# A two-layer hybrid transformer trunk on one core: Strassen's form for the first MLP product of layer 0

## The chip, the core and the metric

The kernel runs on 1 core of one Trainium2 chip. The metric is the device time of one execution in microseconds (us); of several runs the median is taken. Engines: PE is TensorE (matmuls; PEld its weight loads), DVE is VectorE, ACT is ScalarE, POOL is GpSimd, SP is SyncE, which here issues nearly all DMAs. SBUF is the on-chip memory that all engines read, PSUM the memory that matmuls write.

## What is computed

Two layers of a trunk of width 1024 over 512 noised (latent) tokens and 256 context tokens. Cut to what matters here:

```python
for l in range(2):
    m_lat, m_ctx = silu(c) @ w_mod[l] + b_mod[l], silu(c_ctx) @ w_mod[l] + b_mod[l]   # 6 x 1024 each
    h = modulate(rmsnorm(x), sh1, sc1)            # latent and context each with their own
    x = x + ga1 * (concat(attention(h), gated_mlp(h)) @ w_out[l])
    h = modulate(rmsnorm(x), sh2, sc2)
    x = x + ga2 * (square(relu(h @ w_ff1[l])) @ w_ff2[l])     # 1024 -> 4096 -> 1024
return x_lat                                       # in layer 1 only the latent part goes on after attention
```

The change concerns the last line of layer 0, over all 768 tokens: `h @ w_ff1` is called the first product, the one with `w_ff2` the second.

## The kernel before

All activations lie feature-major: 8 tiles of 128 features x 768 tokens. Matmuls are 128x128 weights by up to 512 tokens in fp32r. For precision each operand is split into a rounded part hi (a cast on ACT, L207) and the rest lo (a subtraction on DVE, L208), and each product takes three matmuls: hi·hi, hi·lo, lo·hi. A token run of 768 is done in two halves of 384, so that an output tile of the first product (8 feature blocks, 3 matmuls, 2 halves) takes 48 matmuls of 128x384.

**Weights.** Blocks of 128x1024 come in a fixed order (`block_order`): a DMA on SP's queue into one of two raw buffers, a split into a ring of 4 hi and 4 lo slots (`pump`, `split`). `take` hands a block to its user, `release` frees it, and later `settle` pumps the next.

**Layer 0's MLP.** The 32 hidden tiles are made in 8 chunks of 4 and live in eight units of SBUF, B0 to B6 and C0. `ff1` (L986) makes one tile: 48 matmuls into a PSUM tile pa, then `relu2`: Relu on ACT (L954), Square on ACT (L959) to hi, a square (L960) and a subtraction (L961) on DVE to lo. The second product of a chunk (`proj4`, L786) takes the four hidden tiles, makes 8 output tiles m0 to m7 (24 matmuls each, in turn in pa, or in pb and pt), and each is added to the residual X with the modulation's gate on DVE (`gate`, L784: 384 columns of the first half, then 128 and 256 of the second). The tiles of chunk c+1 are made around the second product of chunk c: one ahead of it, three behind. So each chunk has 384 matmuls, 192 for either product.

**Beside it.** `mod_wide` (L347) computes layer 1's modulation, without PE: 128x512 blocks of w_mod come by DMA, ACT multiplies by the condition (L365, L368), POOL adds (L369); DVE transposes and sums (L380, L381). The MLP calls `more()` to emit a piece of it at a time. `consts(1)` (L550) loads layer 1's small constants and builds its rotary tables (L563, L564); it is called after `ff1_first`, the first chunk of layer 0.

**Order.** In chunks 0 to 6 the instructions of DVE and ACT keep the order in which the program is written (`manual_schedule`, "DA"); a scheduler orders those of PE, POOL and SP, and in chunk 7 all of them. An instruction waits for its inputs on its own engine's queue, and all behind it wait with it. The program's waits on PSUM go by whole tiles.

## Time and profile before

| | |
|---|---|
| median of 3 runs | 1532.02 us (1531.33 to 1533.99) |
| span of the profiled execution | 1530.9 us |
| the stretch of layer 0's MLP taken for the stage | 433 to 911 us |
| instructions | 22786 |

The page gives, for the slowest (here the only) core, each engine's busy time, the chain of work that ended last, and groups of instructions by source line, engine, operation and tile names (`out<-in`). Matmuls are pipelined, so that the row of one shows more (0.33 us) than the distance to the next. Waits are put down to what came last before the waiting instruction began.

### The profile page before, as it was taken

To read this page: it belongs to the slowest core of one execution; us is meant where nothing else is said; L and a number is where in the kernel's file an instruction comes from. 1 tells how busy PE (TensorE), PEld (TensorE's weight loads), DVE (VectorE), ACT (ScalarE), POOL (GpSimd) and SP (SyncE) were. 2 spreads that over 40 slices of the span, in tenths; PEclk is the share of its full clock that TensorE was granted. 3 is DMA by queue.
4 is the path that set the end of the run, shared out by engine and by line. 5 is a ranking of instruction groups with operands and counts; after the bars stand their busy time and mean duration, and the time that the engine had idled before them with its cause. 6 is when DMAs were issued, how large, how long until landed. Compare 5 with 4: busy or idle time off the path is not lost.

```text
span 1530.9 us, 22786 instructions
## 1 busy us (share of the span) xinstructions
PE 1484.1 (97%) x8804; PEld 1321.5 (86%) x8804; DVE 957.4 (63%) x1874; ACT 682.6 (45%) x1142; POOL 402.0 (26%) x362
## 2 busy tenths in 40 slices
PE   6999899999999999999999999998999999999998
PEld 2899686779899999999999998996889888888887
DVE  5868966776855555555555547988796644444443
ACT  3542355564545453545444424535784433322221
POOL 0112320023244545545454603035213000000000
PEclk9999999999999999999999999999999999999999
DMA  9221324321134333333333321221101333332332
GB/s 359 67 74 48 119 91 152 110 83 56 62 108 122 113 123 126 111 118 106 124 109 124 98 68 56 86 80 44 41 1 56 97 96 97 98 97 97 96 98 79
DMA packets 49948, 148.83 MB, mean 97 GB/s; under 512 B 5424, under 2 KB 6832, under 8 KB 49840
## 3 DMA queue, kind: packets, MB, share of 16 engines
q1 hardware_dynamic: 49264, 146.46, 29.9%
q8 instruction: 69, 1.13, 0.3%
q10 hardware_dynamic: 576, 0.92, 0.2%
q14 instruction: 39, 0.32, 0.1%
HBM read 145.26 MB, written 2.10 MB: 96 GB/s over the span
## 4 chain that ended last, share of the span: by engine, by line
PE 82%; DVE 12%; DMA 2%; ACT 2%; issue 1%; POOL 0%; SPq 0%; ACTq 0%; POOLq 0%; DVEq 0%
PE pa L203 51%; PE pb L203 21%; PE pt L844 3%; PE pt L203 3%; PE pb L326 2%; DVE lo L208 1%; DMA X<-in_xT 1%; DMA C<-in_w_mod 1%; DVE X L784 1%; DMA A<-in_w_mod 1%; DVE m L277 1%; PE pt L626 1%; DVE B L961 1%; ACT hi L207 1%; PE pb L865 0%
## 5 line engine op out<-in xcount | busy, mean ns | idle before, releaser
L203 PE MATMUL pa<-A,hi 128*128 128x384 f32 (+2 forms) x1696 | 449.2, 347 | 1.7 <-ACT w L954 0.6
L207 ACT CAST hi<-raw 128x1024 fp32r<-128x1024 f32 x171 | 179.5, 1050 | 409.9 <-PE pa L203 326.3
L208 DVE TENSOR_TENSOR lo<-raw,hi 128x1024 fp32r<-128x1024 f32 x155 | 202.7, 1308 | 215.8 <-ACT hi L207 212.4
L203 PEld LDWEIGHTS pa<-A,hi 128*128 128x128 f32 x1696 | 304.7, 188 | 25.9 <-ACT w L954 1.8
L369 POOL TENSOR_TENSOR C<-C,s 128x512 f32<-128x512 f32 x168 | 240.5, 1463 | 245.0 <-ACT s L368 244.8
L203 PE MATMUL pa<-A,lo 128*128 128x384 f32 (+2 forms) x848 | 293.4, 347 | 1.1 <-DVE lo L208 1.1
L203 PE MATMUL pa<-B,hi 128*128 128x384 f32 (+1 forms) x900 | 246.4, 356 | 4.4 <-DVE X L784 4.4
L203 PEld LDWEIGHTS pa<-B,hi 128*128 128x128 f32 x900 | 162.9, 188 | 21.5 <-DVE X L784 9.2
L784 DVE SCALAR_TENSOR_TENSOR X<-pa,modT,X 128x384 f32<-128x384 f32 (+1 forms) x168 | 88.0, 547 | 143.0 <-PE pa L203 143.0
L203 PEld LDWEIGHTS pa<-A,lo 128*128 128x128 f32 x848 | 159.3, 188 | 12.0 <-DVE lo L208 1.3
L203 PE MATMUL pa<-B,lo 128*128 128x384 f32 (+1 forms) x450 | 158.1, 353 | 0.0
L203 PE MATMUL pb<-B,hi 128*128 128x256 f32 (+2 forms) x600 | 152.3, 340 | 0.4 <-DVE X L784 0.4
L368 ACT ACTIVATE s<-k,silu 128x512 f32<-128x512 f32 x168 | 114.3, 716 | 49.4 <-DMA k<-in_w_mod 27.3
L203 PE MATMUL pb<-hi,A 128*128 128x256 f32 x672 | 126.1, 285 | 0.0
L784 DVE SCALAR_TENSOR_TENSOR X<-pb,modT,X 128x512 f32<-128x512 f32 (+3 forms) x116 | 69.1, 602 | 75.8 <-PE pb L203 75.3
L203 PEld LDWEIGHTS pb<-B,hi 128*128 128x128 f32 x600 | 104.0, 189 | 11.6 <-DVE X L784 1.0
L203 PEld LDWEIGHTS pb<-hi,A 128*128 128x128 f32 x672 | 106.1, 191 | 0.2 <-issue 0.2
L203 PE MATMUL pb<-B,lo 128*128 128x256 f32 (+2 forms) x300 | 101.5, 338 | 0.0
L203 PE MATMUL pb<-lo,A 128*128 128x256 f32 x336 | 95.3, 284 | 0.0
L203 PEld LDWEIGHTS pa<-B,lo 128*128 128x128 f32 x450 | 84.4, 188 | 5.8
L847 DVE TENSOR_TENSOR A<-pt,A 128x384 fp32r<-128x384 f32 (+1 forms) x144 | 73.6, 535 | 16.4 <-ACT A L846 14.4
L846 ACT CAST A<-pt 128x384 fp32r<-128x384 f32 (+1 forms) x144 | 64.6, 469 | 43.3 <-PE pt L844 39.5
(169 smaller groups left out, 2300.3 us busy)
## 6 DMA issues: line engine op xcount, KB each, us to landing
raw<-in_w_ff SPq DMA_DIRECT2D x128, 512.0 KB, 3.5
k<-in_w_mod SPq DMA_DIRECT2D x96, 256.0 KB, 3.0
hi<-in_w_mod SPq DMA_DIRECT2D x32, 512.0 KB, 3.6
raw<-in_w_tok SPq DMA_DIRECT2D x19, 512.0 KB, 3.5
raw<-in_w_out SPq DMA_DIRECT2D x16, 512.0 KB, 3.5
A<-in_w_mod SPq DMA_DIRECT2D x8, 512.0 KB, 9.9
raw<-in_w_u SPq DMA_DIRECT2D x8, 512.0 KB, 3.5
B<-in_w_mod SPq DMA_DIRECT2D x6, 512.0 KB, 10.2
```

The source lines that it names most:

```text
L203: pe.matmul(out, a, b, start=start, stop=stop)
L207: act.copy(hi, src)
L208: (eng or vec).tensor_tensor(out=lo, in0=src, in1=hi.bitcast(F32), op=ALU.subtract)
L277: vec.tensor_scalar(yi, v.bitcast(I32), -0.5, 1595932665.0, op0=ALU.mult, op1=ALU.add)
L326: pe.matmul(ps[q:q + 32, :], S32[:, k, :], w[:, k2 * 512:(k2 + 1) * 512], start=k < ns, stop=k >= KT - ns)
L368: act.activation(p, w, AF.Copy, scale=s)
L369: pool_e.tensor_tensor(out=a, in0=a, in1=p, op=ALU.add)
L626: pe.transpose(p[:, o:o + 128], stk[:, t, hh, c0:c0 + 128].bitcast(F32), ident)
L784: vec.scalar_tensor_tensor(out=xs, in0=src[:, s - off:e - off], scalar=modT[l][:, i * 8 + m, cond:cond + 1], in1=xs, op0=ALU.mult, op1=ALU ...
L844: pe.transpose(tp_[:, (kt - k0) * 128:(kt - k0) * 128 + 128], p[:, kt * 128:kt * 128 + 128], ident)
L846: act.copy(pth[:, k0:k0 + step, d], src)
L847: vec.tensor_tensor(out=ptl[:, k0:k0 + step, d], in0=src, in1=pth[:, k0:k0 + step, d].bitcast(F32), op=ALU.subtract)
```

## The change

In layer 0, chunks 1 to 7, the first product is made in pairs of hidden tiles (p, p + 16) by Strassen's scheme in Winograd's form: the two tiles' weights are split into 2 x 2 blocks of 4 x 128 rows (A11, A12 of tile p, A21, A22 of tile p + 16), the tokens into two halves of 384 and the features into two halves of four blocks (B11 to B22). Instead of 8 block products, 7 are taken (12 matmuls of 128x384 each), of sums of blocks. Chunk 0 is made as before, from tiles 0, 16, 1, 17, and w_ff2's rows are re-ordered on the host to match.

- `factor` makes the weight factors one ring slot at a time: al (the raw A11, A12), be (S2 and S1), ga (what has become of A11 and A12), q (a half slot of its own). POOL computes them in place by four additions of 128x512 (L288 to L291) on the raw buffer and on a second buffer in unit B6 or C0. 3.5 blocks are split for each pair instead of 2.
- `factors` makes the token sums, once, issued under chunk 0's second product: 8 additions of 128x768 on POOL (hi + lo, L1085), 16 differences on DVE (L1096), 16 hi on ACT, 8 lo on DVE and 8 on POOL (L1098). They are kept in units B0 to B5 and in the token half of the first four h tiles that they replace.
- `ff1_pair` (L1120) takes the 7 products in PSUM halves A and C (one pa tile), B (pb) and E (pt), and combines them on ACT and DVE. Its products in order: A1 (al), C1 (be), A2 (al), B1 (be), E (q), B2 (ga), C2 (ga). `c1_` and `c5` are copies of A1 and C1 out of PSUM.
- Hidden tiles now lie in four units, H0 to H3, which at other times hold other data (layer 1's constants in H2 and H3), so both pairs of a chunk are made ahead of its second product, and none runs a chunk ahead. `proj4` with `early` does the first half of the contraction for m0 to m2 first.
- `consts(1)` is called at the end of chunk 7.
- `mod_wide` leaves out the context condition for the column blocks j from 4 on, which layer 1 doesn't use: 112 additions on POOL instead of 168. Its last step is put off by 6000 ns of the emission clock, and `more()` is called at other places (none in chunk 0's second product).

In the whole program there are 168 matmuls of 128x384 fewer (2976, then 2808), 122 more tensor_tensor and 42 more scalar_tensor_tensor on DVE, 86 more casts and 92 fewer activations on ACT, 30 more tensor_tensor on POOL, and as many DMAs (335).

```diff
+        if l == 0:
+            o += [("ff1", l, m) for m in (0, 16, 1, 17)]
+            for ch in range(8):
+                if ch:
+                    a, b = 2 * ch, 2 * ch + 1
+                    o += [("al", l, a), ("be", l, a), ("al", l, b), ("ga", l, a), ("be", l, b), ("ga", l, b)]
+                o += [("ff2", l, ch, nb) for nb in range(4)]
+            continue
...
+    def factor(key):
+        kind, l, p = key
+        hi, lo = slot()
+        if kind == "al":
+            ra = ring.tile([128, 1024], F32, tag="raw", name=nm("raw"), bufs=2)
+            nc.sync.dma_start(ra, w_ff1[l, p])
+            rb = unit(("B6", "C0")[p % 2], [128, 1536], F32)
+            nc.sync.dma_start(rb[:, 512:1536], w_ff1[l, p + 16])
+            raws[p] = ra, rb
+            split(hi, lo, ra)
+            a11, a12, s2, a21, a22 = ra[:, 0:512], ra[:, 512:1024], rb[:, 0:512], rb[:, 512:1024], rb[:, 1024:1536]
+            tt = pool_e.tensor_tensor
+            tt(out=a11, in0=a11, in1=a21, op=ALU.subtract)
+            tt(out=a21, in0=a21, in1=a22, op=ALU.add)
+            tt(out=s2, in0=a22, in1=a11, op=ALU.subtract)
+            tt(out=a12, in0=a12, in1=s2, op=ALU.subtract)
+        elif kind == "be":
+            split(hi, lo, raws[p][1][:, 0:1024])
+        else:
+            ra, rb = raws.pop(p)
+            split(hi, lo, ra)
+            qh, ql = (ring.tile([128, 512], F32R, tag=t, name=nm(t), bufs=1) for t in ("qh", "ql"))
+            split(qh, ql, rb[:, 1024:1536])
+            ready.append((("q", l, p), qh, ql))
+        ready.append((key, hi, lo))
...
+            conds = range(2 if j < 4 else 1)
...
+                    if early and pi == 0 and m < 3:
+                        if m == 0:
+                            wbs.update((i, take(*keys, i)) for i in range(2))
+                            ew = [w4(wbs[i // 2], i, R) for i in range(3)]
+                            if len(parts) > 1:
+                                ed = [pa(), None, pa()]
+                                ed = [[p[:, 0:512], p[:, 512:1024]] if p is not None else [pb(), pt()] for p in ed]
+                            else:
+                                p = pa()
+                                ed = [[p[:, 0:512]], [p[:, 512:1024]], [pb()]]
+                            for i in range(3):
+                                for q, (off, n) in enumerate(parts):
+                                    fm_mms(ed[i][q][:, 0:n], ew[i], off, n, 0, 2)
+                                fl.tick()
+                        for q, (off, n) in enumerate(parts):
+                            fm_mms(ed[m][q][:, 0:n], ew[m], off, n, 2, 4)
+                            gate(i_, m, off, n, ed[m][q])
+                            if post:
+                                post(m, off)
+                            if pi == len(passes) - 1 and q == len(parts) - 1 and m % 2:
+                                release()
+                            yield
+                        continue
...
+        strassen = l == 0
+        hn = TQ // 2
+        def hidden(m):
+            H[m] = unit(f"H{(m % 2) + m // 16 * 2}" if strassen else hslots[m % 8], [128, 2, T])
...
+        def factors():
+            ux = [unit(f"B{i}", [128, 2, 2, 384]) for i in range(6)]
+            def tokens(k):
+                hv = []
+                for kk in (k, k + 4):
+                    v = tw([128, TQ])
+                    pool_e.tensor_tensor(out=v, in0=h2[kk][:, 0, 0:TQ].bitcast(F32), in1=h2[kk][:, 1, 0:TQ].bitcast(F32), op=ALU.add)
+                    hv.append(v)
+                return hv
+            for k in range(4):
+                hv = tokens(k)
+                b11, b12, b21, b22 = hv[0][:, 0:hn], hv[0][:, hn:TQ], hv[1][:, 0:hn], hv[1][:, hn:TQ]
+                dst = [h2[k][:, :, hn:TQ]] + [ux[(k * 3 + i) // 2][:, (k * 3 + i) % 2] for i in range(3)]
+                TT.append(dst)
+                t = [None] * 4
+                for i, (x, y) in ((0, (b12, b11)), (1, (b22, 0)), (3, (b21, 1)), (2, (b22, b12))):
+                    t[i] = tsm([128, hn])
+                    vec.tensor_tensor(out=t[i], in0=x, in1=t[y] if isinstance(y, int) else y, op=ALU.subtract)
+                    act.copy(dst[i][:, 0], t[i])
+                    (pool_e if i > 1 else vec).tensor_tensor(out=dst[i][:, 1], in0=t[i], in1=dst[i][:, 0].bitcast(F32), op=ALU.subtract)
+                    yield
...
+        def put(m, j, sq):
+            hi, lo = (H[m][:, a, j * hn:(j + 1) * hn] for a in range(2))
+            act.copy(hi, sq)
+            vec.tensor_tensor(out=lo, in0=sq, in1=hi.bitcast(F32), op=ALU.subtract)
+        def sqrelu(t):
+            vec.scalar_tensor_tensor(out=t, in0=t, scalar=0.0, in1=t, op0=ALU.max, op1=ALU.mult)
+            return t
...
+        def ff1_pair(p):
+            hidden(p)
+            hidden(p + 16)
+            quad = lambda j, n: lambda k: tuple(h2[j * 4 + k][:, a, n * hn:(n + 1) * hn] for a in range(2))
+            tsum = lambda i: lambda k: tuple(TT[k][i][:, a, 0:hn] for a in range(2))
+            ps = pa()
+            A, C = ps[:, 0:hn], ps[:, 512:512 + hn]
+            B, E = pb()[:, 0:hn], pt()[:, 0:hn]
+            cc = tw([128, 2, hn])
+            uu = tw([128, 2, hn])
+            c1_, c5 = cc[:, 0], cc[:, 1]
+            U2, U3 = uu[:, 0], uu[:, 1]
+            tt = vec.tensor_tensor
+            al = take("al", l, p)
+            product(A, al, 0, quad(0, 0), True, True)
+            act.copy(c1_, A)
+            be = take("be", l, p)
+            product(C, be, 512, tsum(0), True, True)
+            act.copy(c5, C)
+            more()
+            product(A, al, 512, quad(1, 0), False, True)
+            release()
+            r = tsm([128, hn])
+            act.activation(r, A, AF.Relu)
+            hd = H[p]
+            act.activation(hd[:, 0, 0:hn], r, AF.Square)
+            tt(out=r, in0=r, in1=r, op=ALU.mult)
+            tt(out=hd[:, 1, 0:hn], in0=r, in1=hd[:, 0, 0:hn].bitcast(F32), op=ALU.subtract)
+            more()
+            product(B, be, 0, tsum(1), True, True)
+            release()
+            tt(out=U2, in0=B, in1=c1_, op=ALU.add)
+            more()
+            product(E, take("q", l, p), 0, tsum(3), True, True)
+            ga = take("ga", l, p)
+            product(B, ga, 0, tsum(2), False, True)
+            tt(out=U3, in0=B, in1=c1_, op=ALU.add)
+            pool_e.tensor_tensor(out=c5, in0=c5, in1=U3, op=ALU.add)
+            t21 = tsm([128, hn])
+            tt(out=t21, in0=E, in1=U3, op=ALU.add)
+            put(p + 16, 0, sqrelu(t21))
+            more()
+            product(C, ga, 512, quad(1, 1), False, True)
+            release()
+            tt(out=U2, in0=C, in1=U2, op=ALU.add)
+            put(p, 1, sqrelu(U2))
+            put(p + 16, 1, sqrelu(c5))
+            more()
...
-        if not last:
-            K1.append(consts(l + 1))
...
-                    ff1(ch * 4 + 4)
-                    more()
-                R = [H.pop(ch * 4 + kk) for kk in range(4)]
+                if strassen:
+                    if ch:
+                        ff1_pair(2 * ch)
+                        ff1_pair(2 * ch + 1)
+                    R = [H.pop(m) for m in (2 * ch, 2 * ch + 16, 2 * ch + 1, 2 * ch + 17)]
+                    sums = factors() if ch == 0 else iter(())
+                else:
+                    if ch < 7:
+                        ff1(ch * 4 + 4)
+                    R = [H.pop(ch * 4 + kk) for kk in range(4)]
+                    sums = iter(())
...
-                for n, _ in enumerate(proj4(("ff2", l, ch), R, 5, passes, "b" if end else "a", post)):
+                for n, _ in enumerate(proj4(("ff2", l, ch), R, 5, passes, "b" if end else "a", post, early=ch and strassen)):
                     fl.tick()
-                    if n % 2 == 1 and not end:
+                    next(sums, None)
+                    if n % 2 == 1 and not end and ch:
                         more()
-                if not end:
+                for _ in sums:
+                    pass
+                if strassen:
+                    if end:
+                        K1.append(consts(l + 1))
+                elif not end:
                     for i in range(1, 4):
                         ff1(ch * 4 + 4 + i)
-                        more()
```

**DVE, the second product of a middle chunk.** Of the changed kernel, from the gates of tile m3 (X_2, pa_7409) to those of m5 (X_3, pb_7487 and pt_7488); L840 is the gate, L216 the subtraction of `split`; raw_7439 with B_1298 are the two buffers of the next pair a.

```order
L840 SCALAR_TENSOR_TENSOR X_2_75<-pa_7409,modT_88,X_2_75 128x384
L840 SCALAR_TENSOR_TENSOR X_2_75<-pa_7409,modT_88,X_2_75 128x128
L840 SCALAR_TENSOR_TENSOR X_2_75<-pa_7409,modT_88,X_2_75 128x256
L216 TENSOR_TENSOR lo_7438<-raw_7439,hi_7437 128x1024
L216 TENSOR_TENSOR lo_7450<-B_1298_7441,hi_7449 128x1024
L840 SCALAR_TENSOR_TENSOR X_3_76<-pa_7456,modT_88,X_3_76 128x384
L840 SCALAR_TENSOR_TENSOR X_3_76<-pa_7456,modT_88,X_3_76 128x128
L840 SCALAR_TENSOR_TENSOR X_3_76<-pa_7456,modT_88,X_3_76 128x256
L840 SCALAR_TENSOR_TENSOR X_3_76<-pb_7487,modT_88,X_3_76 128x384
L840 SCALAR_TENSOR_TENSOR X_3_76<-pt_7488,modT_88,X_3_76 128x128
```

The same place before, from m3's first gate (pa_5632) on:

```order
L784 SCALAR_TENSOR_TENSOR X_2_75<-pa_5632,modT_88,X_2_75 128x384
L208 TENSOR_TENSOR lo_5649<-raw_5646,hi_5648 128x1024
L784 SCALAR_TENSOR_TENSOR X_2_75<-pa_5632,modT_88,X_2_75 128x128
L784 SCALAR_TENSOR_TENSOR X_2_75<-pa_5632,modT_88,X_2_75 128x256
L784 SCALAR_TENSOR_TENSOR X_3_76<-pa_5673,modT_88,X_3_76 128x384
L784 SCALAR_TENSOR_TENSOR X_3_76<-pa_5673,modT_88,X_3_76 128x128
L784 SCALAR_TENSOR_TENSOR X_3_76<-pa_5673,modT_88,X_3_76 128x256
L784 SCALAR_TENSOR_TENSOR X_3_76<-pb_5708,modT_88,X_3_76 128x384
L208 TENSOR_TENSOR lo_5726<-raw_5723,hi_5725 128x1024
L784 SCALAR_TENSOR_TENSOR X_3_76<-pt_5709,modT_88,X_3_76 128x128
```

The lo's of al and of be now stand together between m3's gates and m4's, where single lo's of other blocks stood between the gates of one tile.

**PE, the same place.** Of the changed kernel, from the last matmuls of the early part of m6 (pa_7519) on; pb_7594 is the product B1 of the next pair, hi_7449 and lo_7450 are be, pa_7456 is tile m4:

```order
L211 MATMUL pa_7519<-H_1266_7157,hi_7351 128x384 x2
L211 MATMUL pa_7519<-H_1266_7157,lo_7352 128x384
L1116 MATMUL pb_7594<-B_959_4799,hi_7449 128x384 x2
L1116 MATMUL pb_7594<-B_959_4799,lo_7450 128x384
L1116 MATMUL pb_7594<-B_960_4800,hi_7449 128x384 x2
L1116 MATMUL pb_7594<-B_960_4800,lo_7450 128x384
L211 MATMUL pa_7456<-H_1244_6999,hi_7255 128x384 x2
L211 MATMUL pa_7456<-H_1244_6999,lo_7256 128x384
L211 MATMUL pa_7456<-H_1245_7000,hi_7255 128x384 x2
L211 MATMUL pa_7456<-H_1245_7000,lo_7256 128x384
```

Before, where the matmuls of one output tile follow on those of the tile ahead:

```order
L203 MATMUL pa_5673<-B_1050_5299,lo_5433 128x384
L203 MATMUL pa_5673<-C_1060_5374,hi_5432 128x384 x2
L203 MATMUL pa_5673<-C_1060_5374,lo_5433 128x384
L203 MATMUL pb_5708<-B_989_4834,hi_5432 128x384 x2
L203 MATMUL pb_5708<-B_989_4834,lo_5433 128x384
L203 MATMUL pb_5708<-B_1037_5218,hi_5432 128x384 x2
L203 MATMUL pa_5673<-B_989_4834,hi_5432 128x384 x2
L203 MATMUL pa_5673<-B_989_4834,lo_5433 128x384
L203 MATMUL pa_5673<-B_1037_5218,hi_5432 128x384 x2
L203 MATMUL pa_5673<-B_1037_5218,lo_5433 128x384
```

The first half of the next pair's B1 stands before the second half of m4. Between the last matmul of m3 and the first of B1 are 20 matmuls of m4 and m6.

**ACT, from pair a to pair b of a chunk.** Of the changed kernel: s_7064 is the Relu of pair a's tile, H_1244 and H_1245 its hidden tiles, hi_7100 and hi_7104 be and ga of pair b, L418 products of the modulation, w_7161<-pa_7158 the copy of pair b's A1:

```order
L1144 ACTIVATE s_7064<-pa_7001 128x384
L1146 ACTIVATE H_1244_6999<-s_7064 128x384
L418 ACTIVATE C_1255_7040<-k_5166,silu 128x512 x2
L215 CAST hi_7100<-C_1243_6977 128x1024
L215 CAST hi_7104<-raw_6975 128x1024
L215 CAST qh_7108<-C_1243_6977 128x512
L1104 CAST H_1245_7000<-s_7126 128x384
L418 ACTIVATE C_1255_7040<-k_5166,silu 128x512
L1104 CAST H_1244_6999<-w_7005 128x384
L1104 CAST H_1245_7000<-w_7004 128x384
L418 ACTIVATE C_1255_7040<-k_5166,silu 128x512
L1136 COPY w_7161<-pa_7158 128x384
```

Before, between two `ff1` tiles and their splits:

```order
L207 CAST hi_7192<-raw_7190 128x1024
L954 ACTIVATE w_7196<-pa_7133 128x768
L959 ACTIVATE B_1289_7134<-w_7196 128x768
L207 CAST hi_7260<-raw_7258 128x1024
L954 ACTIVATE w_7264<-pa_7205 128x768
L959 ACTIVATE B_1299_7206<-w_7264 128x768
L365 ACTIVATE C_1306_7275<-k_4859,silu 128x512 x2
L368 ACTIVATE s_7280<-k_4859,silu 128x512
L368 ACTIVATE s_7283<-k_4859,silu 128x512
L368 ACTIVATE s_7313<-k_4859,silu 128x512
L368 ACTIVATE s_7316<-k_4859,silu 128x512
```

The copy of pair b's first product stands behind three splits, the three casts of pair a's hidden tiles and four products of the modulation, where one split and the two activations of a tile stood.

More of the change, by code (lines that the diff above doesn't have):

```diff
@@ L263, in take @@
     def take(*key):
-        if not ready:
+        if not any(e[0] == key for e in ready):
             settle()
-        k, hi, lo = ready.pop(0)
-        assert k == key, (k, key)
+        i = [e[0] for e in ready].index(key)
+        assert i == 0 or key[0] in ("be", "ga", "q", "al"), (key, ready[0][0])
+        k, hi, lo = ready.pop(i)
         return hi, lo
@@ L360, in mod_wide @@
                 load(j * KT + k + 1)
-                for cond in range(2):
+                for cond in conds:
                     a, s = acc[:, cond, :], sc[:, k, cond:cond + 1]
@@ L375, in mod_wide @@
                     yield
-            part = small(32).rearrange("p (c b) -> p c b", c=2)
-            for cond in range(2):
+            part = small(32, tag="pa", bufs=2).rearrange("p (c b) -> p c b", c=2)
+            for cond in conds:
                 tr = tsm([128, 512])
@@ L866, in third @@
                     fl.vt += 220.0
-                t = tmp.tile([64, 256], F32, tag="pv", name=nm("pv"), bufs=1)
+                t = st["mix"][0:64, 256:512]
                 act.copy(t, o[64:128, 0:256])
@@ new lines, in put, with product @@
+        def put(m, j, sq):
[5 more added lines that the diff above has]
+            return t
+        def product(dst, w, wo, rhs, first, last_):
+            for k in range(4):
+                whi, wlo = (a[:, wo + k * 128:wo + k * 128 + 128] for a in w)
+                rhi, rlo = rhs(k)
+                for i, (a, b) in enumerate(((whi, rhi), (whi, rlo), (wlo, rhi))):
+                    pe.matmul(dst, a, b, start=first and k == 0 and i == 0, stop=last_ and k == 3 and i == 2, skip_group_check=True)
+                    fl.vt += hn / 2.4 + 13.0
+            fl.tick()
```

78 lines of the change are left out of this document (47 added, 31 removed), and 2 rows, old and new, of the table PAR.

## The prediction

> **What bounds the kernel now.** I read the page first (busy shares, then the chain that ended last), then the busy time of the stage that the change touches, then the waits of that stage, then single rows.
>
> ```profile
> PE 1484.1 (97%) x8804; PEld 1321.5 (86%) x8804; DVE 957.4 (63%) x1874; ACT 682.6 (45%) x1142; POOL 402.0 (26%) x362
> PE 82%; DVE 12%; DMA 2%; ACT 2%; issue 1%; POOL 0%; SPq 0%; ACTq 0%; POOLq 0%; DVEq 0%
> ```
>
> TensorE is busy for 97% of the span, and 82% of the chain lies on it. The window view of layer 0's MLP (columns: stretch, its length, busy time and instructions of PE, PEld, DVE, ACT, POOL, then the granted clock, DMA share, GB/s):
>
> ```profile
> 433.00:911.00 478.00, 473.22 (x2762) 462.45 (x2760) 256.32 (x347) 224.69 (x300) 236.96 (x166) 1.00 0.36 114
> ```
>
> Here PE is busy for 473.22 of 478 us, at a full clock, while DVE, ACT and POOL have about half of their time free. So a matmul removed is worth its whole time, as long as nothing else makes PE wait. The view of waits says who waits for whom (total us, times, longest), and a timeline row shows the longest wait of PE in this stage:
>
> ```profile
> POOL C L369 <- ACT s L368: 226.8, 37, 22.1
> ACT hi L207 <- PE pa L203: 139.6, 39, 8.4
> DVE lo L208 <- ACT hi L207: 112.6, 34, 6.2
> DVE X L784 <- PE pa L203: 97.1, 59, 2.9
> PE pa L203 <- DVE X L784: 4.4, 5, 1.2
> ...
> 713.76 0.62 PE L203 MATMUL pa<-B,hi 128*128 128x384 f32 x2 [1.18 <-DVE X L784]
> ```
>
> Everybody waits for PE; PE waits five times, 4.4 us in all. The splits (hi on ACT, lo on DVE) are made whole chunks ahead. That lead is what the change spends.
>
> **What it removes.** 14 pairs take 7 products of 12 matmuls instead of 8: 168 matmuls of 128x384 fewer (2976 before, 2808 after). Their price, from a run without a gap:
>
> ```profile
> 699.76 0.33 PE L203 MATMUL pa<-A,lo 128*128 128x384 f32 x1
> ...
> 707.04 0.33 PE L203 MATMUL pa<-A,lo 128*128 128x384 f32 x1
> ```
>
> Between these two rows lie 14 triples of matmuls, 42 in 7.28 us, so 0.1733 us each. 168 x 0.1733 = **29.1 us removed**, all on the path.
>
> **The first handover (weight factor be).** Durations for this and the next part, from the groups by form (count, then busy us, mean ns, idle before):
>
> ```profile
> L208 DVE TENSOR_TENSOR lo<-raw,hi 128x1024 fp32r<-128x1024 f32 x55 | 79.8, 1450 | 102.3 <-ACT hi L207 102.3
> L207 ACT CAST hi<-raw 128x1024 fp32r<-128x1024 f32 x55 | 57.6, 1048 | 141.6 <-PE pa L203 127.4 <-PE pt L203 14.1
> L369 POOL TENSOR_TENSOR C<-C,s 128x512 f32<-128x512 f32 x166 | 237.0, 1459 | 226.9 <-ACT s L368 226.8
> L743 POOL TENSOR_TENSOR C<-s,C 128x512 f32<-128x512 f32 x10 | 12.8, 1287 | 26.0 <-DVE s L739 19.6 <-DVE m L285 6.1 <-DVE mv L716 0.4
> L784 DVE SCALAR_TENSOR_TENSOR X<-pa,modT,X 128x256 f32<-128x256 f32 x42 | 19.9, 475 | 0.0
> L784 DVE SCALAR_TENSOR_TENSOR X<-pa,modT,X 128x128 f32<-128x128 f32 x42 | 14.7, 351 | 83.3 <-PE pa L203 83.3
> ```
>
> The order puts al's lo on DVE behind the gates of tile m3 of the running second product. POOL overwrites raw in place, so its three adds for be wait for that lo; then comes be's hi on ACT, then be's lo on DVE. From the end of m3's matmuls: two gates 0.35 + 0.48, lo 1.45, three adds at 1.29 (the shorter of the two POOL rows, that of work outside the modulation) 3.86, hi 1.05: 7.2 us. In PE's order 20 matmuls stand between m3's end and the first matmul that reads be: 3.5 us. PE waits 3.7, then be's lo (1.45) is waited for behind two matmuls (0.35): 1.1 more, so about 4.8; I take 4.9 for the semaphores between. On DVE m4's gates are queued behind be's lo, and PE's second half of m4 waits for them; that is inside the same wait. Lower end 4.3: both lo's at 1.23, the shortest I saw. Upper end 6.5: adds at 1.459, both lo's held by POOL. It occurs in chunks 1 to 6: 6 x 4.9 = **29.4 us** (26 to 39).
>
> ```profile
> 931.83 1.23 DVE L208 TENSOR_TENSOR lo<-raw,hi 128x1024 fp32r<-128x1024 f32 x1
> ```
>
> **The second handover (pair a to pair b).** More rows; L846 and L847 are the nearest to a copy and to a subtraction of 128x384 out of PSUM, L368 is one modulation product:
>
> ```profile
> L847 DVE TENSOR_TENSOR A<-pt,A 128x384 fp32r<-128x384 f32 x128 | 67.0, 549 | 12.7 <-ACT A L846 10.7
> L846 ACT CAST A<-pt 128x384 fp32r<-128x384 f32 x128 | 58.6, 481 | 35.7 <-PE pt L844 31.9 <-PE pb L203 2.3
> L368 ACT ACTIVATE s<-k,silu 128x512 f32<-128x512 f32 x166 | 112.8, 716 | 48.0 <-DMA k<-in_w_mod 27.3 <-POOL C L369 20.4
> L207 ACT CAST B<-s 128x512 fp32r<-128x512 f32 x10 | 6.2, 618 | 11.0 <-DVE s L721 11.0
> L960 DVE TENSOR_TENSOR w<-w 128x512 f32<-128x512 f32 x32 | 22.1, 691 | 0.0
> ACT s L368 <- DMA k<-in_w_mod: 27.3, 19, 2.8
> ```
>
> C1 of pair b writes the PSUM tile that A1 of pair b shares, so it waits until ACT has copied A1. That copy stands on ACT behind pair a's tail. From the end of A2 of pair a: Relu and Square 2 x 0.48, two modulation products 1.43, the wait for their DMA 0.7 (half of 27.3 us by 19), be's hi 1.05: 4.1. Then DVE: three lo's 1.45 + 1.45 + 0.75 (the last, q's, has half the columns), two operations at 0.55 and a square at 0.6: 9.5. Then to and fro: ACT cast 0.48, DVE lo, addition and square 1.7, cast 0.48, lo and square 1.15, cast 0.48, one product 0.72, the copy 0.48: 15.0 us. PE has 68 matmuls from A2 of a to C1 of b, 11.8 us. The difference is 3.2; I take 3.0, since a lo and a cast can overlap by a little; ends 0 and 6. Chunk 7 isn't held to the written order of ACT and DVE, so 6 x 3.0 = **18.0 us** (0 to 36).
>
> **Smaller waits.** C1 of pair a stands right behind A1 and waits for one ACT copy, 0.48 and its signals: 0.6 x 7 = 4.2. After C2 of pair b its tail takes DVE 0.55 + 0.6, ACT 0.48, DVE 0.55 + 0.6, ACT 0.48, DVE 0.55 = 3.8 us, with two lo's of the second product's weights (2.9) queued between on DVE and signals: 6.9. The early half of the second product covers it with 36 matmuls, 6.2 us; 0.7 x 7 = 4.9 are left (0 to 17). Only H0 to H3 hold hidden tiles now, so no first product runs ahead that could fill any of this.
>
> **The token sums.** They are POOL's and DVE's, beside chunk 0's second product.
>
> ```profile
> L775 POOL TENSOR_TENSOR A<-C,A 128x768 fp32r<-128x768 f32 x2 | 4.1, 2062 | 1.5 <-ACT A L774 1.5
> L208 POOL TENSOR_TENSOR B<-mix,B 128x256 fp32r<-128x256 f32 x8 | 5.9, 734 | 12.4 <-ACT B L207 12.4
> L961 DVE TENSOR_TENSOR B<-w,B 128x768 fp32r<-128x768 f32 x23 | 35.7, 1553 | 0.8
> L960 DVE TENSOR_TENSOR w<-w 128x768 f32<-128x768 f32 x27 | 25.8, 956 | 9.8 <-ACT B L959 9.0 <-ACT C L959 0.7
> 641.72 7.12 POOL L369 TENSOR_TENSOR C<-C,s 128x512 f32<-128x512 f32 x5 [1.67 <-ACT s L368]
> 642.04 1.93 DVE L961 TENSOR_TENSOR B<-w,B 128x768 fp32r<-128x768 f32 x1
> ```
>
> POOL: 8 adds of 128x768 at 2.06, 8 lo's of 128x384 at 1.5 x 0.73 = 1.1, 8 factor adds at 1.29: 35.6 us. DVE: 16 differences and 8 lo's at half of 0.956 plus a start, 0.52, and three splits at 1.45: 16.9. Does the one run beside the other? Here L961 and L960 have the same shape on the same engine, and L961, which runs under POOL's adds as at 642.04, takes 1553 ns against 956. So at least a part is serial. If all of it is, 52.5 us stand against 40.9 of PE work (192 matmuls of the second product and 44 of the next pair that need no sums): 11.6 late; if none, 0. I take **10** (0 to 20), near the serial end as L961 is; m2 to m7's gates stand behind the sums in DVE's order and hold PE's PSUM.
>
> The Trainium skill ("SBUF — State Buffer", section "SBUF: two separate sides") says that a DVE operation with two SBUF inputs and a GpSimd operation reading SBUF take a shared port as an exclusive lock, one fully blocking the other. By that rule the term would be 11.6; the trace agrees in direction (L961, 1553 ns against 956).
>
> **The constants of layer 1** move to the end of chunk 7, since H2 and H3 must be free.
>
> ```profile
> k<-in_pk ACTq DMA_DIRECT2D x2, 320.0 KB, 3.5
> L563 DVE TENSOR_TENSOR G<-w,k 128x128 f32<-128x128 f32 x8 | 2.2, 280 | 0.0
> ```
>
> A 3.5 us DMA and 11 DVE operations of 0.28, 3.1 us, then stand ahead of layer 1's first sinks on DVE; some is covered by the norm there: **3** (0 to 7). Costed at nothing: the modulation's 56 fewer POOL adds and as many ACT products fewer (neither bounds the stage), 122 more DVE tensor_tensors where DVE is free, the re-ordered rows of w_ff2 (same bytes), the same 335 DMAs on SP's queue.
>
> **The sum.** 29.4 + 18.0 + 4.2 + 4.9 + 10 + 3 = 69.5 lost, 29.1 gained: +40.4. The profiled span is 1530.9, so 1571.3; the median (1532.02) lies 1.1 above the span, so **1572.4 us**. The ends: with every lower end 26 + 0 + 4 + 0 + 0 + 0 - 29 = +1, 1533; with every upper end 39 + 36 + 4 + 17 + 20 + 7 - 29 = +94, 1626.
>
> **Rivals.** *Both handovers hidden (faster).* If be's hi is there when PE reaches it, and pair a's tail is done in time, with the sums hidden beside chunk 0, 4.2 + 4.9 + 3 - 29.1 = -17: 1515. For it: DVE and ACT are half idle, and before, PE waited 4.4 us in all. Against: the chains above are of dependences, not of load. It decides for faster as soon as the two handovers with the sums cost under 17 us, so under 1.2 us per handover. 0.22, a mistake of mine in the order's slack included.
>
> *POOL holds DVE everywhere (slower still).* POOL now runs factor adds beside every lo. With 6.5 and 5 per handover, 15 for the sums, 8 and 5 for tail and constants: 39 + 30 + 4.2 + 8 + 15 + 5 - 29 = +72: 1604. For: L961. Against: L208's mean of 1450 already has some of it. 0.14.
>
> *The clock falls after each wait.* The granted clock is 1.00 in the window above, whose longest PE wait is 1.18 us; no run here shows a wait of 5. Were the 12 matmuls after each first handover at half clock, 6 x 12 x 0.1733 = 12.5 more: 1585. 0.06. The Trainium skill ("TensorE: Matmul & The Clock Gate", "What's actually happening") names an idle window of about 3.4 us after which the clock halves; by that rule this rival is on.
>
> *The saving is not there, or exactly eaten* (+-0.2%, 3 us, is what a measurement of this kernel can tell from no change): 0.04. The forecast has 0.54.
>
> **Numbers.** Faster 0.22, same 0.04, slower 0.54 + 0.14 + 0.06 = 0.74. The forecast's own range is 1550 to 1605; the range for 8 in 10 reaches from 1512, within the faster rival, to 1606, beyond the POOL rival's value.
>
> **What would show it.** In the profile after: PE waits of 4 to 5 us in front of the product on pb, put down to ACT's or DVE's hi or lo of be, once per chunk from 1 to 6; shorter ones of about 3 us in front of C1 of pair b, put down to ACT's copy; PE busy time down by about 29 us in this stage; DVE lo's above 1.45 us under POOL's adds. Wrong if PE's waits in the stage sum to under 29 us, if be's hi begins before m3's last gate, or if the chunk period falls below 68 us.

## The result, and the profile after

The changed kernel takes 1640.77 us (median of 4 runs, 1640.33 to 1641.15) against 1531.9 of the kernel before: 1.0705 times as long, 95% interval 1.069 to 1.0721. It is slower by 108.9 us, where 40 were forecast, and it lies above the forecast's range. Its profiled span is 1639.2 us.

The page after, busy shares and the chain that ended last:

```profile
span 1639.2 us, 22575 instructions
PE 1506.8 (92%) x8636; PEld 1320.4 (81%) x8636; DVE 1025.0 (63%) x2022; ACT 669.4 (41%) x1164; POOL 432.8 (26%) x392
PE 65%; DVE 19%; ACT 6%; DMA 4%; POOL 3%; issue 3%; DVEq 0%; SPq 0%; POOLq 0%; ACTq 0%
```

TensorE's share of the chain has gone from 82% to 65%: work of DVE, ACT and POOL now lies between matmuls. PE's busy time has risen, from 1484.1 to 1506.8 us, with 168 matmuls fewer. That is the first sign of slower matmuls. The windows of the stage (columns as in the prediction; the last number but two is the granted clock), three of them here, each from its second product's handover to the next one's:

```profile
554.00:644.00 90.00, 73.01 (x376) 68.24 (x376) 47.65 (x71) 37.84 (x58) 50.74 (x39) 0.90 0.30 94
725.00:805.00 80.00, 69.64 (x376) 65.41 (x376) 42.97 (x67) 27.97 (x43) 32.00 (x25) 0.95 0.32 106
805.00:886.00 81.00, 70.81 (x377) 66.59 (x376) 42.92 (x68) 27.88 (x43) 32.00 (x24) 0.92 0.32 104
```

A chunk takes 80 to 90 us, against 68.7 before, and the clock is 0.90 to 0.95, where it was 1.00. The waits of PE in the stage, 433 to 968 us:

```profile
PE pa L1116 <- ACT w L1136: 36.1, 12, 7.0
PE pb L1116 <- ACT hi L215: 25.2, 8, 3.5
PE pa L211 <- DVE X L840: 9.3, 5, 3.2
PE pa L1116 <- DVE X L840: 5.2, 7, 0.9
PE pb L1116 <- DVE lo L216: 5.2, 7, 1.6
PE pa L211 <- ACT H L1104: 1.5, 2, 0.8
```

The two largest are the handovers of the prediction: ACT's copy of A1 (L1136) in front of C1, and be's hi in front of B1.

To divide the 108 us I took the distance between the starts of successive matmuls, from the layer's MLP to the end, less the distance at full clock (0.1733 us for 384 columns, 0.2267 for 512, 0.1193 for 256). What is left over counts as a wait where the trace shows PE idle for more than 0.1 us, and as slowness elsewhere. The three terms add up to 106.6 of the 108 us:

| from 381 us on | matmuls at full clock | waits | slowness |
|---|---|---|---|
| before | 1063.4 | 19.0 | 25.8 |
| changed | 1035.4 | 112.7 | 66.7 |
| difference | -28.0 | +93.7 | +40.9 |

The saving is there (29.1 forecast). Of the slowness, 26.1 us are 178 matmuls that follow one another at 0.32 us instead of 0.173 (before: hardly any). The trace's record of the granted clock says why: between 433 and 975 us it has 15 stretches at 0.50, each 3.41 or 6.83 us long, one in or behind each wait of 2.5 us or more; in the stage of the kernel before it has none. Two of them as windows:

```profile
725.72:729.11 3.39, 3.39 (x12) 3.39 (x12) 0.19 (x1) 0.72 (x1) 2.94 (x3) 0.50 0.45 153
804.22:811.03 6.81, 6.47 (x19) 5.96 (x20) 1.82 (x2) 2.16 (x4) 4.55 (x4) 0.50 0.38 118
```

Nearly all matmuls at 0.32 us start within such stretches, and all matmuls that start within them account for 31 of the 40.9 us. The remaining 9 or so lie at full clock. A part of them is the first matmul behind each wait, which is followed by the next after 0.25 or 0.28 us (after 0.48 at half clock); the others are spread and were not traced to a cause.

**The first handover in the trace.** Timeline rows of DVE, POOL, ACT and PE (start, length):

```profile
717.15 0.74 DVE L840 SCALAR_TENSOR_TENSOR X<-pa,modT,X 128x128 f32<-128x128 f32 x2 [2.67 <-PE pa L211]
717.81 1.22 DVE L216 TENSOR_TENSOR lo<-raw,hi 128x1024 fp32r<-128x1024 f32 x1
...
724.07 1.32 DVE L216 TENSOR_TENSOR lo<-B,hi 128x1024 fp32r<-128x1024 f32 x1 [5.04 <-ACT hi L215]
```

```profile
719.11 1.29 POOL L288 TENSOR_TENSOR raw<-raw,B 128x512 f32<-128x512 f32 x1 [5.56 <-DVE lo L216]
720.48 1.26 POOL L289 TENSOR_TENSOR B<-B 128x512 f32<-128x512 f32 x1
721.70 1.26 POOL L290 TENSOR_TENSOR B<-B,raw 128x512 f32<-128x512 f32 x1
```

```profile
722.99 1.05 ACT L215 CAST hi<-B 128x1024 fp32r<-128x1024 f32 x1 [9.94 <-POOL B L290]
```

```profile
724.09 0.61 PE L1116 MATMUL pb<-B,hi 128*128 128x384 f32 x2 [3.50 <-ACT hi L215]
725.44 0.48 PE L1116 MATMUL pb<-B,lo 128*128 128x384 f32 x1 [0.74 <-DVE lo L216]
725.72 0.84 PE L1116 MATMUL pb<-B,hi 128*128 128x384 f32 x2
726.36 0.52 PE L1116 MATMUL pb<-B,lo 128*128 128x384 f32 x1
...
729.36 0.52 PE L211 MATMUL pa<-H,hi 128*128 128x384 f32 x2
729.72 0.34 PE L211 MATMUL pa<-H,lo 128*128 128x384 f32 x1
```

Read across the engines, it is the forecast chain, link by link: m3's gates, al's lo, three additions, be's hi, 6.9 us from 717.15 to the end of be's hi at 724.04 (forecast 7.2), and behind it be's lo. Then read the last fence down: between 725.72 and 726.36 two matmuls start, 0.32 us each; from 729.36 to 729.72 it is again two, but 0.18 us each.

**The second handover.** ACT and DVE between A2 of pair a and the copy of pair b's A1, then PE:

```profile
746.45 0.49 ACT L1144 ACTIVATE s<-pa 128x384 f32<-128x384 f32 x1 [1.24 <-PE pa L1116]
...
748.74 1.44 ACT L418 ACTIVATE C<-k,silu 128x512 f32<-128x512 f32 x2 [1.24 <-DMA k<-in_w_mod]
...
757.10 0.51 ACT L1104 CAST H<-s 128x384 fp32r<-128x384 f32 x1 [4.51 <-DVE s L1108]
...
760.09 0.51 ACT L1104 CAST H<-w 128x384 fp32r<-128x384 f32 x1 [1.85 <-DVE w L1108]
761.70 0.51 ACT L1104 CAST H<-w 128x384 fp32r<-128x384 f32 x1 [1.09 <-DVE w L1108]
762.11 0.72 ACT L418 ACTIVATE C<-k,silu 128x512 f32<-128x512 f32 x1
762.74 0.46 ACT L1136 COPY w<-pa 128x384 f32<-128x384 f32 x1
```

```profile
751.21 2.15 DVE L216 TENSOR_TENSOR lo<-C,hi 128x1024 fp32r<-128x1024 f32 x1 [2.06 <-POOL C L419]
753.28 1.21 DVE L216 TENSOR_TENSOR lo<-raw,hi 128x1024 fp32r<-128x1024 f32 x1
...
758.70 1.36 DVE L1108 SCALAR_TENSOR_TENSOR w<-w 128x384 f32<-128x384 f32 x1
```

```profile
758.16 0.34 PE L1116 MATMUL pt<-B,ql 128*128 128x384 f32 x1
763.25 1.01 PE L1116 MATMUL pa<-A,hi 128*128 128x384 f32 x2 [4.75 <-ACT w L1136]
```

ACT idles 4.51 us, and the copy, whose product ended at 754, stands behind three casts that wait for DVE. The chain is 16.8 us (746.45 to 763.20), forecast 15.0. The two DVE operations that ran longest, 2.15 and 1.36 against 1.21 and 0.55 for their like, began while POOL was adding. In chunks 1 and 2, with both conditions of the modulation, this wait is 7.0 us.

### The profile page after: what moved, and what is told of

The parts are those of the page before. It is cut to its first block, busy times and chain, and to the rows that moved or that the text cites. A ratio compares the mean times of both kernels' runs of the same rounds, so it can differ in the third digit from the quotient of the medians.

```text
span 1639.2 us, 22575 instructions
## 1 busy us (share of the span) xinstructions
PE 1506.8 (92%) x8636; PEld 1320.4 (81%) x8636; DVE 1025.0 (63%) x2022; ACT 669.4 (41%) x1164; POOL 432.8 (26%) x392
## 4 chain that ended last, share of the span: by engine, by line
PE 65%; DVE 19%; ACT 6%; DMA 4%; POOL 3%; issue 3%; DVEq 0%; SPq 0%; POOLq 0%; ACTq 0%
PE pa L211 32%; PE pb L211 18%; PE pa L1116 5%; DVE lo L216 4%; PE pt L924 2%; PE pt L211 2%; PE pb L373 2%; PE pb L1116 2%; DMA k<-in_w_mod 2%; ACT hi L215 1%; DVE X L840 1%; POOL C L419 1%; DMA X<-in_xT 1%; ACT C L418 1%; DVE w L1108 1%
## 5 line engine op out<-in xcount | busy, mean ns | idle before, releaser
L216 DVE TENSOR_TENSOR lo<-raw,hi 128x1024 fp32r<-128x1024 f32 x155 | 199.4, 1290 | 138.6 <-ACT hi L215 135.2
L211 PE MATMUL pa<-A,hi 128*128 128x512 f32 (+2 forms) x800 | 220.5, 361 | 3.0 <-DVE B L708 1.4
L211 PE MATMUL pa<-H,hi 128*128 128x384 f32 (+1 forms) x688 | 191.2, 359 | 12.8 <-DVE X L840 9.3
L840 DVE SCALAR_TENSOR_TENSOR X<-pa,modT,X 128x384 f32<-128x384 f32 (+1 forms) x170 | 89.2, 548 | 145.3 <-PE pa L211 145.2
L1116 PE MATMUL pa<-A,hi 128*128 128x384 f32 x448 | 126.3, 365 | 42.1 <-ACT w L1136 36.1
L419 POOL TENSOR_TENSOR C<-C 128x512 f32<-128x512 f32 x84 | 115.4, 1374 | 143.3 <-ACT C L418 142.0
L211 PEld LDWEIGHTS pa<-H,hi 128*128 128x128 f32 x688 | 131.7, 201 | 23.3 <-DVE X L840 11.6
L211 PE MATMUL pa<-A,lo 128*128 128x512 f32 (+2 forms) x400 | 143.8, 361 | 1.1 <-DVE lo L216 1.1
L211 PE MATMUL pa<-H,lo 128*128 128x384 f32 (+1 forms) x344 | 118.5, 351 | 0.0
L840 DVE SCALAR_TENSOR_TENSOR X<-pb,modT,X 128x512 f32<-128x512 f32 (+3 forms) x114 | 67.6, 599 | 68.9 <-PE pb L211 68.4
L211 PE MATMUL pb<-B,hi 128*128 128x512 f32 (+1 forms) x404 | 101.2, 341 | 0.1
L211 PE MATMUL pa<-B,hi 128*128 128x512 f32 x300 | 92.4, 389 | 0.0
L1116 PE MATMUL pb<-B,hi 128*128 128x384 f32 x224 | 63.6, 366 | 26.5 <-ACT hi L215 25.2
L211 PEld LDWEIGHTS pa<-A,lo 128*128 128x128 f32 x400 | 75.2, 189 | 12.2 <-DVE lo L216 1.3
```

The lines of the kernel that those rows point to most:

```text
L211: pe.matmul(out, a, b, start=start, stop=stop)
L216: (eng or vec).tensor_tensor(out=lo, in0=src, in1=hi.bitcast(F32), op=ALU.subtract)
L419: pool_e.tensor_tensor(out=a, in0=a, in1=p, op=ALU.add)
L840: vec.scalar_tensor_tensor(out=xs, in0=src[:, s - off:e - off], scalar=modT[l][:, i * 8 + m, cond:cond + 1], in1=xs, op0=ALU.mult, op1=ALU ...
L1116: pe.matmul(dst, a, b, start=first and k == 0 and i == 0, stop=last_ and k == 3 and i == 2, skip_group_check=True)
```

## The experiments

The theories. **Order**: PE waits because each engine works in its written order, and chains of dependent work stand in front of what PE needs. **Clock**: a wait of some 3 us also halves the speed of the matmuls behind it. **POOL**: POOL's additions hold DVE, and their amount decides. Times are medians; each run was timed beside the kernel before on the same chip.

**be without al's lo** (e1_be_free).

```diff
-            tt(out=a11, in0=a11, in1=a21, op=ALU.subtract)
             tt(out=a21, in0=a21, in1=a22, op=ALU.add)
-            tt(out=s2, in0=a22, in1=a11, op=ALU.subtract)
+            tt(out=s2, in0=a21, in1=a11, op=ALU.subtract)
+            tt(out=a11, in0=a22, in1=s2, op=ALU.subtract)
             tt(out=a12, in0=a12, in1=s2, op=ALU.subtract)
```

> The changed kernel with the weight factors summed in another order: S1 = A21 + A22 and S2 = S1 - A11 first, and only then A11 and A12 overwritten, so that be needs two POOL additions instead of three and does not wait for al's lo. Same number of additions. In the changed kernel PE waits 3.3 to 3.5 us for be's hi and 0.7 for its lo in chunks 1 to 6, 25 us in all. Order theory (waits alone cost): those waits fall to under 1 us each, 1640.8 - 22 = about 1619 us. Clock theory (a wait of over 3 us is followed by some 10 matmuls at half speed, 1.5 to 2.4 us): 12 us more, about 1607. POOL theory (POOL's additions hold DVE, and their number decides): under 5 us gained, above 1635.

1617.48 us, ratio 1.0555 (1.0539 to 1.057). PE's waits in the stage:

```profile
PE pa L1116 <- ACT w L1136: 42.9, 12, 8.1
PE pa L211 <- DVE X L840: 12.0, 9, 3.3
PE pb L1116 <- DVE lo L216: 3.8, 6, 1.6
...
PE pb L1116 <- ACT hi L215: 0.6, 1, 0.6
```

The row of be's hi falls from 25.2 to 0.6 us: with the same additions on POOL, two of them before be and no wait for al's lo. So the first handover came from the order of the sums. 23 us were gained, but not in the way that order alone would have it: in the division above, waits fell by only 14.7 us, because the second handover took 7 back (36.1 to 42.9), and slowness fell by 9.3.

**Pair b's A1 and C1 ahead of pair a's tail** (e2_a1_ahead).

```diff
             tt(out=t21, in0=E, in1=U3, op=ALU.add)
+            ahead = ff1_start(nxt_) if nxt_ else None     # A1, copy, C1, copy of pair b
             put(p + 16, 0, sqrelu(t21))
```

> The changed kernel with the first two products of pair b (A1, C1) and their copies out of PSUM written ahead of pair a's tail, so that ACT makes the copies before the tail's casts. Nothing else. In the changed kernel PE waits 7.0 us in front of C1 of pair b in chunks 1 and 2 and 4.5 to 5.4 in chunks 3 to 6, 33.5 us in all. Order theory: that goes, less 1 us or so per chunk: 1640.8 - 28 = about 1613 us. Clock theory: 1.6 us per chunk more, about 1603. POOL theory: the tail only moves and the wait comes back in front of a later product: above 1630.

1630.82 us, ratio 1.0644 (1.0626 to 1.0661):

```profile
PE pb L1116 <- ACT hi L215: 23.4, 8, 3.5
PE pa L211 <- DVE X L840: 18.4, 12, 4.3
PE pa L1116 <- ACT s L1148: 13.6, 6, 5.6
...
PE pa L1116 <- ACT w L1130: 4.9, 10, 1.0
```

The wait for the copy (now L1130) fell from 36.1 to 4.9 us, but 13.6 came back in front of the next product, for pair b's Relu (L1148), and 9 at the gates. A third of the expected gain is left. The time is the one that I had written down for POOL, yet the waits name ACT's and DVE's queues, so it does not settle which.

**Both** (e12_both).

> Both edits together. Order theory: 1640.8 - 22 - 28 = about 1591 us. Clock theory: no wait of over 3 us is left in chunks 2 to 7, so the half-speed matmuls go too (5 to 6 us per chunk): 1570 us or less, granted clock above 0.99 in these chunks. POOL theory: above 1620. Below 1532 would need the token sums and all small waits to cost under 29 us together.

1604.52 us, ratio 1.0466 (1.045 to 1.0481). It lies between what the order theory and what the POOL theory expected, and far above what the clock theory did. The edits add up (23.3 + 10.0, and 36.3 together). In two chunks:

```profile
704.00:779.00 75.00, 67.32 (x376) 61.97 (x376) 46.04 (x69) 28.25 (x42) 32.47 (x24) 1.00 0.34 113
779.00:853.00 74.00, 67.15 (x376) 61.99 (x376) 45.00 (x68) 28.25 (x42) 32.55 (x24) 1.00 0.34 112
```

Here no wait is over 2 us and the clock is 1.00 again; a chunk takes 74.5 us, 6 less than after the change and 6 more than before it.

**More work in the wait** (e3_keep_warm).

```diff
             act.copy(c1_, A)
+            if p % 2 and p < 15:
+                for _ in range(2):
+                    product(B, al, 0, quad(0, 0), True, True)
             be = take("be", l, p)
```

> The changed kernel with work added: in pair b of chunks 1 to 6 the first product A1 is taken twice more into the PSUM tile of B, which the real product then overwrites: 24 matmuls, 4.2 us each time, 25 us of TensorE work in all, placed by the scheduler between A1 and the wait in front of C1. The wait ends with ACT's copy, which the added matmuls don't move. Order theory: the added work takes the place of the wait, 1641 us (same). Clock theory: the wait left is too short for the clock to fall, and the 10 half-speed matmuls behind it (1.5 us) go: about 1631 us, faster with more work. If the added work is not hidden: 1650 to 1666.

1641.35 us, ratio 1.0706 (1.0687 to 1.0725): 144 more matmuls, 25 us, cost nothing. That shows how much room the waits are. The clock's part of the expectation failed: the waits left at the two handovers are 2.3 to 3.3 us in chunks 3 to 6, in front of C1 still 7.0 and 5.0 in chunks 1 and 2, and 173 matmuls still ran at 0.32 us.

So I counted, over the eleven profiles of the changed kernel and the ten experiments here, what follows a wait of PE in this stage:

| wait of PE, us | waits | followed by three or more matmuls at 0.32 us |
|---|---|---|
| 0.4 to 1 | 268 | 21 |
| 1 to 2 | 78 | 12 |
| 2 to 2.9 | 41 | 28 |
| 2.9 and more | 64 | 63 |

Those that follow, from 2.9 on, are 11 to 14 on the mean: 12 x 0.147 = 1.8 us on top of each wait. In the first two rows some waits stand close behind a longer one, or several short ones together.

The clock records say what decides between 2 and 2.9 us. In each run all half-clock stretches lie on one grid of steps of 3.41 us, whose phase differs from run to run. Over these eleven profiles and the one before, from 381 us on, I summed PE's idle time within each step of the grid that ran at full clock. All 109 steps with 1.9 us or more were followed by half clock, 11 of 43 with 1.5 to 1.9 us, and none of 3944 with less. So a wait of 2 to 3 us costs extra or not by where it falls on the grid. The Trainium skill ("TensorE: Matmul & The Clock Gate", section "What's actually happening") gives an idle window of about 3.4 us before the clock halves, and calls it free-running. These traces agree on the window's length and on its running free of the program; by them it need not be idle throughout, as 1.9 us were enough.

**The context condition's products on DVE** (e4_ctx_on_dve): both edits and

```diff
-"MP": [0, 1]
+"MP": [0]
```

> Both edits of the run before, and the modulation's products of the context condition (chunks 1 and 2 alone have them) made by DVE's scalar_tensor_tensor instead of an ACT product and a POOL addition. In the run with both edits PE still waits 6.7 and 7.7 us for pair b's Relu, which on ACT stands behind four such products that wait for POOL, and 4.3 us twice behind the second product's gates. Modulation theory (ACT and POOL are overrun while two conditions are made): these waits fall to the size of chunks 3 to 6 (1.7 and 0.9), 16 us, and 6 us of half-speed matmuls with them: 1604.5 - 22 = about 1582 us. If they come from the order alone: no change, 1600 to 1606.

1603.74 us, ratio 1.0465 (1.0448 to 1.0482): no change. The waits for the Relu in chunks 1 and 2 shrank from 6.7 and 7.7 to 5.1 and 4.4 us, and at the gates the wait of 4.3 became one of 2.8 with new ones of 0.4 to 1.6 beside it, behind DVE's products. Taking this load off ACT and POOL gained nothing, as it cost as much on DVE.

**All of the modulation's products on DVE** (e5_mod_on_dve: both edits, `"MP": []`; e7_after_mod_dve: the changed kernel's own order, `"MP": []`).

> As the kernel before it, but all products of the modulation on DVE, so that POOL has only the factor and token additions and ACT none of the products. POOL theory: the lo's of the splits fall to 1.2 us each and the tail of a pair with them; waits in front of C1, A2 and C2 of pair b go: 1560 us or less. Order theory: the products now stand in DVE's order ahead of the tail and the gates, 18 a chunk of 0.7 to 0.8 us, and with them the waits for their DMA: no better than the kernel before it, 1580 to 1600.

> The changed kernel in its own order, but all products of the modulation on DVE (no ACT product, no POOL addition for it). Order theory: the first handover stays (4.2 us in chunks 1 to 6); the second loses two or three ACT products and one DMA wait, 2 us, and gains as many products on DVE: 1630 to 1645. POOL theory: DVE's lo's and subtractions are no longer held, both handovers shrink by 2 to 3 us each, in chunks 1 and 2 by 5: 1600 to 1610.

1612.83 us, ratio 1.0514 (1.0497 to 1.0532), and 1647.97 us, ratio 1.0748 (1.0732 to 1.0764): both slower than their parents. The groups of one sort of lo in the stage, in the changed kernel and then in e7:

```profile
L216 DVE TENSOR_TENSOR lo<-C,hi 128x1024 fp32r<-128x1024 f32 x6 | 10.9, 1820 | 18.4 <-ACT hi L215 7.4 <-POOL C L419 6.9 <-issue 4.1
```

```profile
L216 DVE TENSOR_TENSOR lo<-C,hi 128x1024 fp32r<-128x1024 f32 x6 | 7.3, 1218 | 0.0
```

```profile
PE pa L211 <- DVE X L840: 26.1, 28, 2.6
PE pa L1116 <- ACT w L1136: 24.9, 12, 5.7
PE pb L1116 <- ACT hi L215: 21.0, 6, 3.7
```

POOL's additions do hold DVE (1820 against 1218 ns). The Trainium skill ("SBUF — State Buffer", section "SBUF: two separate sides") says that a DVE operation with two SBUF inputs and a GpSimd operation that reads SBUF block each other on a shared port; these rows agree in direction. Taking 109 of the additions away bought that back, and the second handover fell from 36.1 to 24.9 us; but the products then stood in DVE's queue ahead of the gates, and those waits rose from 9.3 to 26.1. As the main cause POOL has fallen with e1, where the same additions ran and 23 us were gained. e5 and e7 show only that moving its work to DVE is no remedy; what POOL's hold costs by itself was not measured.

**Token sums on DVE** (e6_sums_on_dve): both edits, `vec` for `pool_e` in `factors`.

> Both edits (be, and pair b ahead), with the token sums and all their lo's on DVE instead of POOL; the factors stay on POOL. In the changed kernel PE waits 9 to 10 us in and behind chunk 0's second product, by gates and by be of pair 1. POOL theory of that stage (the two engines run one after the other): DVE needs 8 x 0.96 + 32 x 0.52 + splits = 29 us beside 33 us of PE work, so the waits fall to 3 us or less: 1604.5 - 7 = about 1598 us. If DVE alone is too slow for it, gates behind the sums: 1604 to 1610.

1607.12 us, ratio 1.0484 (1.0468 to 1.0499): no gain. The waits around chunk 0's second product are 3.1, 2.9, 1.7 and 1.5 us at its gates, where with POOL the largest waits were 2.1, 2.1 and 1.6, one of them at a gate. So the sums cost as much when they run on DVE alone, in front of the gates.

**Only the lost lead** (e8_no_lead): the kernel before, with four hidden units in layer 0 (the weights' order follows).

```diff
-            H[m] = unit(hslots[m % 8], [128, 2, T])
+            H[m] = unit(hslots[m % (4 if l == 0 else 8)], [128, 2, T])
...
+                if l == 0:
+                    for i in range(4 if ch else 0):
+                        ff1(ch * 4 + i)
+                        more()
```

> The kernel before, with one thing of the change alone: in layer 0 only four units hold hidden tiles (B0 to B3), so that the four tiles of a chunk are all made ahead of its second product and none runs a chunk ahead. Eight products per pair of tiles as before, no factors, no token sums, no copies. If the lost lead by itself makes PE wait (the second product must wait for the last tile's Relu, Square and lo, 4 us, each chunk): 1532 + 7 x 4, and half-speed matmuls behind it, 1560 to 1570 us. If the chains inside Strassen's form do (order theory as I hold it now): waits of 1 us or less at that place, 1535 to 1543 us.

1540.81 us, ratio 1.0046 (1.0028 to 1.0064): with ordinary products the chunk-ahead lead is worth 7 us, not 100. The largest waits of PE in the stage are then:

```profile
PE pa L207 <- DVE X L788: 4.5, 2, 3.9
PE pa L207 <- DVE B L965: 3.3, 4, 1.0
```

**The modulation out of the pairs** (e9_mod_in_second), on top of e4.

```diff
-                    if n % 2 == 1 and not end and ch:
+                    if not end and ch:
                         more()
```

and four of the five `more()` in `ff1_pair` left out; the pieces are the same.

> As the kernel with both edits and the context condition on DVE (1603.7 us), with the modulation's pieces taken out of the pairs and put into the second product: one per pair instead of five, and one at every step of the second product instead of every other. Same pieces. Order theory: in front of A2 or C2 of pair b (Relu behind products on ACT) 1.7 to 5 us of wait per chunk go, 14 us in all, with the half-speed matmuls of chunks 1 and 2: about 1585 us. If POOL's load near the splits decides: no gain, since the additions now lie beside the lo's of al and be: 1600 or more.

1593.74 us, ratio 1.0392 (1.0373 to 1.041): 10 us of the 18 expected.

```profile
PE pa L211 <- DVE X L840: 32.7, 30, 2.7
PE pt L438 <- DVE pa L431: 9.2, 4, 2.5
```

No wait for ACT's copy or Relu is left above 0.4 us. What is left are 30 waits behind gates, of 1.1 us on the mean, and four in front of the modulation's own small matmuls (L438), 9.2 us. Against the kernel before this version has 28 us of matmuls less, 65 us of waits and 23 of slowness more. It is the fastest with Strassen's form and still 60 us slower than the kernel before. Whether another order would take these 30 waits away was not tried.

## Why the prediction was wrong, point by point

- **What bounds the kernel** was right: PE, and any wait of it is paid in full. e3 shows it from the other side.
- **The saving**, 29.1: 28.0 in the division of the trace.
- **The first handover**, 29.4: mechanism, place and length right. The six waits for be's hi are 3.3 to 3.5 us, with its lo 24 us in all; e1 removed those for hi by their cause.
- **The second handover**, 18.0: right mechanism, wrong size. 33.5 us: 4.5 to 5.4 in chunks 3 to 6 and 7.0 in chunks 1 and 2. The step that failed here is "I take 3.0": in chunks 1 and 2 twice the modulation stands in the chain, which I left out of the sum, and DVE's operations under POOL took up to 0.9 longer each. My upper end, 6 per chunk, would have held it.
- **Smaller waits**, 4.2 and 4.9: 2.6 for the copy in front of C1 and 1.5 for the tail. In their place came waits behind gates that I had at nothing, 14.5 us with those of chunk 0.
- **The token sums**, 10: 9.5 us of waits in chunk 0. That the size came out is in part luck. About 4 of them are gates behind the sums, and in e6 these waits grew with the sums on DVE alone, so the two engines' exclusion is not the whole reason. Another 4.2 are waits for be of the first pair, whose hi stood on ACT behind a cast of the sums.
- **The constants**, 3: from the stage's last gate to layer 1's second norm it is 220.4 us (1056.8 to 1277.2), and was 217.6 (951.3 to 1168.9). The 2.8 us between fit; no run moves the constants alone.
- **The clock** is the step that failed most: the sum puts it at nothing. I had it as a rival at 0.06 and 12.5 us, on one handover only, with "no run here shows a wait of 5", because no wait in the stage before was long enough to show it. But the same trace has longer waits elsewhere, 4.75 us in front of 186.64 and 4.24 in front of 1053.86, and behind both the granted clock is 0.50 (a timeline row and a window):

```profile
1053.86 1.65 PE L203 MATMUL pa<-B,B 128*128 128x512 f32 x4 [4.24 <-ACT w L828]
1052.90:1059.60 6.70, 5.74 (x15) 4.59 (x16) 3.97 (x9) 2.83 (x5) 3.77 (x4) 0.50 0.17 67
```

In the changed kernel the half clock was on at both handovers, 31 of the 40.9 us of slowness; the other 9, of the first matmuls behind waits and of unknown cause, also stood nowhere in the sum. The forecast itself held waits of 4.9 and 3.0 us, so its own working asked for the clock's price in the sum, not beside it.
- **The range** ended at 1606, below the sum of my own upper ends (1626), and with no clock in it.
- **The rivals.** Both handovers hidden: excluded. POOL holds DVE everywhere: it does lengthen single operations, but e1 gained 23 us with the same additions, and in e5, e6 and e7 moving its work to DVE gained nothing. The clock: on, and at both handovers. The saving not there: excluded by the 28.0. None of their times reached the measured one.

Of the 68 us that the forecast was short, 41 are slowness, 15.5 the second handover; the remaining 12 are mostly waits behind gates, less what I had set too high.

## What to carry to other kernels

Where one engine is busy for 97% and the rest wait for it, an edit that takes 4 us of its work per chunk must not lengthen any chain between its instructions by as much: count, at each place where it needs a new result, the chain of the other engines in their written order against the work that it has queued. When such a sum gives a wait of 3 us or more, add the slower matmuls behind it, here 1.8 us each time; and before calling the clock untested, look for long waits in the whole trace, not in the stage alone. Removing a wait at one link shows the next one: three reorderings gained 47 us of 108, each less than the wait that it removed.

## What I had not expected of the hardware

The clock fell behind 63 of 64 waits of 2.9 us and more, for 11 to 14 matmuls, and behind 28 of 41 of 2 to 2.9 us: 1.9 us of idle time within one step of a 3.41 us grid were enough each time. Even a short wait costs a little more than its length: the first matmul behind it is followed after 0.25 or 0.28 us instead of 0.173.
